# High and low halves of x as one moving operand in 44 projections

## The chip, the cores and the metric

One core of a Trainium2 chip. The metric is the device time of one execution in microseconds (us). The engines go by their names in the profile: PE (TensorE, matrix multiplications), PEld (its weight loads), DVE (VectorE), ACT (ScalarE), POOL (GpSimd) and SP (SyncE, which issues the DMAs of the weights). SBUF is the on-chip memory; PSUM holds the results of PE, here in 8 banks of 128 x 512 floats.

## The reference, cut to what matters

Two stacks run one after the other on `x` of 256 positions by 1024 features, two layers each. The first has five branches in each layer (stick-breaking attention, mLSTM, gated MLP, retention, attention to a memory), the second a mixer or a conformer convolution, cross attention to a second memory, and a convolutional feed-forward. In single precision:

```
proj = rms_norm(x, norm_pre) @ w_in            # (256, 1024) @ (1024, d_in), split into 21 parts
y_gm = spatial_gating(gelu(gm_u), gelu(gm_v), ...)   # times silu(gm_z)
q, k = rotary(rt_q), rotary(rt_k)              # retention
...
h = rms_norm_2(x, norm) @ w_up                 # (256, 1024) @ (1024, 6144)
g = causal_dwconv(h[..., :3072], dw_w, dw_b)   # three taps in time
x = x + (gelu(g) * h[..., 3072:]) @ w_down
```

Nearly all the work is products of a 256 x 1024 (or 512) activation with a weight matrix that is read from HBM once.

## The kernel before

Activations lie with features on partitions and the S = 256 positions along the free axis, in chunks of 128 features. To keep single precision on PE, each operand is split into a high and a low part of a reduced format (fp32r): `Operand` (L244) holds `h` and `l`, written by ACT (a rounding copy) and DVE (the rest, by subtraction, L254 and L259). `weights` (L285) brings a weight block by one DMA on SP into a tile of the pool `wraw` (5 tiles) and splits it into `wh` (ACT, L297) and `wl` (DVE, L298), 128x1024 each, of the pool `whl` (4 tiles). The splits carry a higher priority in the scheduler (`ahead`), so that they stand some way ahead of their use.

A product is three matmuls for each chunk k of the inner axis and each block m of 128 output features, all into one PSUM region: `wh` by `xh`, `wh` by `xl`, `wl` by `xh`. In `mm_F` (L302) the weight is the stationary operand (128x128) and x the moving one, 256 columns wide. `proj_F` (L328) runs it for 512 output features: two banks (`psF`), each with two blocks m of 256 columns, two weight tiles for each half of the inner axis, each [128, 2, 512]. After it, DVE multiplies each bank by the row of norms `rb` into SBUF (`scaled_F`, L344, L347). `mm_T` (L314) is the other form, x stationary and weights moving, 512 columns wide (`psT`). Down and output projections use `mm_F` with banks called `psO`.

The banks come from two pools of four, `mbank` (mm) and `bank` (aux), each in rotation: a bank's next user waits until its last reader is done. `mid` is a piece of other work that `proj_F` calls before the second half of its inner axis. Work elsewhere that the change touches: the sigmoid gates with `silu2_F` (L365), the rotations of retention (`rot`, three DVE products out of each bank, L714 to L716), the keys of the memory attention (`kv_k`, L922) and the feed-forward (`conv_ffn`, L1198): for each of 6 slices a `gx` and a `u` projection, then taps, a gelu and the product, and a down projection of the slice before.

Each engine runs its instructions in order. The order on every engine is set when the program is built, by a list scheduler that places instructions by its own estimate of times and the priorities; nothing is reordered on the chip. So an instruction that waits holds up all that stand behind it on its engine.

Of the kernel before, what the change touches and what calls it, by code (L numbers as in the profile page):

```python
# [11 lines left out]
F32 = mybir.dt.float32  # L12
F32R = mybir.dt.float32r
# [5 lines left out]
S = 256  # L19
# [35 lines left out]
def stack_kernel(ctx: ExitStack, tc: tile.TileContext, I: dict, out: bass.AP):  # L55
# [188 lines left out]
    class Operand:  # L244


        def __init__(self, n, pool, tag):
            self.h = pool.tile([128, n, S], F32R, tag=tag + "h", name=tag + "h")
            self.l = pool.tile([128, n, S], F32R, tag=tag + "l", name=tag + "l")

        def put(self, c, src):
            hi, lo = self.h[:, c], self.l[:, c]
# [49 lines left out]
    def mm_F(pss, src, op, k0, n_k, first, last):  # L302

        w = made.pop() if made else weights(src, n_k)
        for m in range(src.shape[1] // 128):
            for k in range(n_k):
                wh, wl = w[k][0][:, m * 128:m * 128 + 128], w[k][1][:, m * 128:m * 128 + 128]
                xh, xl = op.h[:, k0 + k], op.l[:, k0 + k]
                for n, (a, b) in enumerate(((wh, xh), (wh, xl), (wl, xh))):
                    PE.matmul(pss[m // 2][:, m % 2], a, b,  # L310
                              start=(first and m % 2 == 0 and k == 0 and n == 0),
                              stop=(last and k == n_k - 1 and n == 2), skip_group_check=True)

    def mm_T(pss, src, op, k0, n_k, first, last, extra=None):  # L314

        w = weights(src, n_k)
        for t in range(2):
            sl = slice(t * 128, t * 128 + 128)
            for k in range(n_k):
                xh, xl = op.h[:, k0 + k, sl], op.l[:, k0 + k, sl]  # L320
                wh, wl = w[k]
                for n, (a, b) in enumerate(((xh, wh), (xl, wh), (xh, wl))):
                    PE.matmul(pss[t], a, b, start=(first and k == 0 and n == 0),  # L323
                              stop=(last and k == n_k - 1 and n == 2), skip_group_check=True)
                    if extra is not None and n < 2:
                        extra(t, k0 + k, n, a)
# [22 lines left out]
    def F_plain(w, c0, op, rb, name, dst=None, pss=None):  # L349
        if pss is None:  # L350
            pss = proj_F(w, c0, op)
        if dst is None:
            dst = t_f4([128, 4, S], name)
        scaled_F(pss, rb, dst)
        return dst

    def T_plain(w, c0, op, rc, name, dst=None, extra=None):
        pss = proj_T(w, c0, op, extra=extra)
        if dst is None:
            dst = t_f4([128, 2, 512], name)  # L360
        for t in range(2):
            A.activation(dst[:, t], pss[t], AF.Copy, scale=rc[:, t:t + 1])
        return dst

    def silu2_F(w, c0, op, rb, name, pss=None):  # L365

        z = F_plain(w, c0, op, rb, name, pss=pss)
        th = t_f4([128, 4, S], name + "_t")
        A.activation(th, z, AF.Tanh, scale=0.5)
        V.scalar_tensor_tensor(z, th, 1.0, z, op0=ALU.add, op1=ALU.mult)  # L370
        return z
# [111 lines left out]
    def layer(l, nrm, early, kv, late, nxt):  # L483
# [32 lines left out]
        def sb_branch():  # L516
# [35 lines left out]
                                        compare_op=ALU.is_ge, fill=0.0, base=-1,  # L552
                                        channel_multiplier=-1)

            pss_z = proj_F(w, OFF["sb_z"], op, mid=later)
            z = silu2_F(w, OFF["sb_z"], op, rb, "sbz", pss=pss_z)
            o = Operand(4, yop, "y")
            for i in range(2):
                ps = bank([128, 2, S], "ps_sbo")
# [142 lines left out]
        def rt_branch():  # L702
# [3 lines left out]
            V.tensor_tensor(sr, sinF, rb, op=ALU.mult)  # L706

            def rot(c0, name):
                pss = proj_F(w, c0, op)
                q = t_f4([128, 4, S], name)  # L710
                x = t_f4([128, 4, S], name + "_x")
                for i in range(2):
                    sl = slice(2 * i, 2 * i + 2)
                    V.tensor_tensor(q[:, sl], pss[i], bc(cr, 2), op=ALU.mult)  # L714
                    V.tensor_tensor(x[0:64, sl], pss[i][64:128], bc(sr[64:128], 2), op=ALU.mult)
                    V.tensor_tensor(x[64:128, sl], pss[i][0:64], bc(sr[0:64], 2), op=ALU.mult)  # L716
                V.tensor_tensor(q, q, x, op=ALU.add)
                return q

# [46 lines left out]
        def gm_branch(ws):  # L766
# [17 lines left out]
            for t in range(2):  # L784
# [1 line left out]
                                op1=ALU.mult)  # L786
                V.tensor_tensor(v[:, t], v[:, t], lng[:, 0], op=ALU.mult)
                V.tensor_tensor(v[:, t], v[:, t], lng[:, 1], op=ALU.add)
            u = F_plain(w, OFF["gm_u"], op, rb, "gmu")
# [21 lines left out]

        def xa_branch():
            kF, vT = kv()
            qF = F_plain(w, OFF["xa_q"], op, rb, "xaq")
# [106 lines left out]

    def kv_k(op, rb, w, c0):  # L922
        was, ahead[0] = ahead[0], KV_AHEAD
        k = F_plain(w, c0, op, rb, "kF", kvp.tile([128, 4, S], F32, tag="kv", name="kF"))
        ahead[0] = was
        return k

# [270 lines left out]
    def conv_ffn(l, nrm, nxt):  # L1198
# [9 lines left out]

        for n in range(6):
            get = bank if n else mbank  # L1210
            pg = proj_F(wu, 512 * n, op, get=get)
            if n == 0:
                rc, row = nrm.column(), []
            pu = proj_F(wu, 3 * D + 512 * n, op, get=get,
                        mid=None if n else lambda: row.append(row_of(rc, "x")))
            rb = row[0]
            gx = t_f4([128, 4, S], "f_gx")
            scaled_F(pg, rb, gx)
# [5 lines left out]
            u = t_f4([128, 4, S], "f_u")  # L1224
            o = Operand(4, yop, "y")
            for i in range(2):
                sl = slice(2 * i, 2 * i + 2)
                V.tensor_tensor(u[:, sl], pu[i], bc(rb, 2), op=ALU.mult)
# [182 lines left out]
```

## Time and profile before

| | |
|---|---|
| median of 3 runs | 1823.22 us (1822.25 to 1824.26) |
| profiled execution, own time | 1826.32 us |
| its span, first to last instruction | 1824.6 us |
| PE busy | 1788.9 us, 98% of the span |
| PE weight loads | 1666.0 us, 91% |
| DVE busy | 1265.6 us, 69% |
| ACT busy | 958.9 us, 53% |
| POOL busy | 60.8 us, 3% |
| read from HBM | 306.53 MB, 169 GB/s over the span |

An engine's busy time counts the union of its records. Records of matmuls overlap, since a matmul is shown from its start to the modelled end of a pipeline, so the pace of PE is read from starts. An idle engine that is not waited for costs nothing.

### The profile page before, as it was taken

How to read it: one execution, taken by the hardware profiler on the slowest of the kernel's cores; microseconds unless marked ns; L12 is line 12 of the kernel's file. 1: busy time of each engine (PE TensorE's matmuls, PEld its weight loads, DVE VectorE, ACT ScalarE, POOL GpSimd, SP SyncE). 2: the span in 40 equal slices, each digit the busy share in tenths (PEclk: the TensorE clock that was granted, in tenths of full speed). 3: DMA queues.
4: the chain of work that ended last, by engine and by line, in shares of the span. 5: the costliest groups of instructions: out<-in, count | busy, mean ns of one | idle time of the engine just before them, and what ended most of it. 6: DMA issues, size and time to landing. Idle time of an engine off the chain costs nothing. (4 is left out here: it accounts for less than half of the span.)

```text
span 1824.6 us, 30483 instructions
## 1 busy us (share of the span) xinstructions
PE 1788.9 (98%) x12255; PEld 1666.0 (91%) x12255; DVE 1265.6 (69%) x1888; ACT 958.9 (53%) x1369; POOL 60.8 (3%) x91
## 2 busy tenths in 40 slices
PE   8899999999999999999999999999999989999998
PEld 8889998888999898888899998999999989899998
DVE  6587856676667877656657965676669985577666
ACT  5755335554556443455455854455457545455443
POOL 0000001100000100000000000000000000000000
PEclk9999999999999999999999999999999999999999
DMA  7456554666554655467655554455554344355552
GB/s 222 131 167 208 168 174 147 202 206 193 165 173 146 185 176 169 149 197 232 207 169 178 156 169 144 155 181 178 183 183 146 103 133 151 116 180 184 183 184 93
DMA packets 162654, 309.57 MB, mean 170 GB/s; under 512 B 10852, under 2 KB 19504, under 8 KB 162512
## 3 DMA queue, kind: packets, MB, share of 16 engines
q1 hardware_dynamic: 159872, 302.04, 52.7%
q0 software_dynamic: 2128, 5.37, 1.0%
q8 instruction: 96, 1.57, 0.4%
q14 instruction: 46, 0.38, 0.1%
q10 hardware_dynamic: 512, 0.21, 0.1%
HBM read 306.53 MB, written 1.05 MB: 169 GB/s over the span
## 5 line engine op out<-in xcount | busy, mean ns | idle before, releaser
L298 DVE TENSOR_TENSOR wl<-raw,wh 128x1024 fp32r<-128x1024 f32 x558 | 668.6, 1222 | 343.8 <-ACT wh L297 335.4
L297 ACT ACTIVATE wh<-raw 128x1024 fp32r<-128x1024 f32 x558 | 573.2, 1054 | 529.9 <-PE psF L310 178.4
L310 PE MATMUL psF<-xh,wh 128*128 128x256 f32 x1888 | 538.4, 285 | 3.5 <-ACT wh L1302 3.3
L310 PE MATMUL psF<-xh,wl 128*128 128x256 f32 x1888 | 536.1, 284 | 0.8 <-DVE wl L298 0.8
L310 PE MATMUL psF<-xl,wh 128*128 128x256 f32 x1888 | 536.7, 284 | 0.0
L310 PEld LDWEIGHTS psF<-xh,wh 128*128 128x128 f32 x1888 | 363.7, 193 | 4.5 <-ACT wh L1302 3.6
L310 PEld LDWEIGHTS psF<-xl,wh 128*128 128x128 f32 x1888 | 364.0, 193 | 1.5 <-issue 1.0
L310 PEld LDWEIGHTS psF<-xh,wl 128*128 128x128 f32 x1888 | 363.3, 193 | 1.6 <-DVE wl L298 1.4
L310 PE MATMUL psO<-yh,wh 128*128 128x256 f32 x800 | 227.6, 285 | 6.0 <-ACT yh L253 6.0
L310 PE MATMUL psO<-yl,wh 128*128 128x256 f32 x800 | 227.3, 284 | 0.0
L310 PE MATMUL psO<-yh,wl 128*128 128x256 f32 x800 | 227.0, 284 | 0.3 <-DVE wl L298 0.3
L323 PE MATMUL psT<-wl,xh 128*128 128x512 f32 x544 | 216.3, 398 | 0.0
L323 PE MATMUL psT<-wh,xl 128*128 128x512 f32 x544 | 216.0, 397 | 0.0
L323 PE MATMUL psT<-wh,xh 128*128 128x512 f32 x544 | 214.5, 394 | 0.0
L310 PEld LDWEIGHTS psO<-yh,wh 128*128 128x128 f32 x800 | 154.2, 193 | 6.9 <-ACT yh L253 6.7
L310 PEld LDWEIGHTS psO<-yh,wl 128*128 128x128 f32 x800 | 154.3, 193 | 0.5 <-DVE wl L298 0.5
L310 PEld LDWEIGHTS psO<-yl,wh 128*128 128x128 f32 x800 | 154.3, 193 | 0.3
L323 PEld LDWEIGHTS psT<-wl,xh 128*128 128x128 f32 x544 | 102.7, 189 | 21.4
L323 PEld LDWEIGHTS psT<-wh,xl 128*128 128x128 f32 x544 | 102.8, 189 | 20.8
L323 PEld LDWEIGHTS psT<-wh,xh 128*128 128x128 f32 x544 | 102.8, 189 | 19.6
L1114 DVE SCALAR_TENSOR_TENSOR c_h<-c_a,cols,c_h 128x229 f32<-128x229 f32 (+15 forms) x144 | 63.2, 465 | 3.0
L323 PE MATMUL psT<-wl,yh 128*128 128x512 f32 x160 | 62.3, 389 | 0.0
(414 smaller groups left out, 2134.0 us busy)
## 6 DMA issues: line engine op xcount, KB each, us to landing
raw<-in_w_in SPq DMA_DIRECT2D x224, 512.0 KB, 4.3
raw<-in_f_w_up SPq DMA_DIRECT2D x96, 512.0 KB, 4.3
raw<-in_f_w_down SPq DMA_DIRECT2D x48, 512.0 KB, 4.3
raw<-in_w_up SPq DMA_DIRECT2D x40, 512.0 KB, 4.0
raw<-in_c_w_pw SPq DMA_DIRECT2D x24, 512.0 KB, 3.9
raw<-in_ab_w_in SPq DMA_DIRECT2D x20, 512.0 KB, 4.4
raw<-in_w_mem_kv SPq DMA_DIRECT2D x16, 512.0 KB, 3.9
raw<-in_w_out SPq DMA_DIRECT2D x16, 512.0 KB, 3.6
```

What stands on the lines that cost most here:

```text
L297: A.activation(hi, raw, AF.Copy)
L298: V.tensor_tensor(lo, raw, hi.bitcast(F32), op=ALU.subtract)
L310: PE.matmul(pss[m // 2][:, m % 2], a, b, start=(first and m % 2 == 0 and k == 0 and n == 0), stop=(last and k == n_k - 1 and n == 2), skip ...
L323: PE.matmul(pss[t], a, b, start=(first and k == 0 and n == 0), stop=(last and k == n_k - 1 and n == 2), skip_group_check=True)
L1114: V.scalar_tensor_tensor(h[:, j:], a[:, m, 0:S - j], col("c_dw_w_2", (30 - j) * 8 + c), h[:, j:], op0=ALU.mult, op1=ALU.add)
```

## The change

`Operand` puts `h` and `l` side by side in one tile `hl` ([128, n, 2, 256]), so that both halves of a chunk can be read as one row of 512. A new `proj_P` uses it: for each (k, m), `wh` is multiplied with `hl` (512 columns, into a whole bank: the product with the high part in half 0, with the low part in half 1), and `wl` with `h` (256 columns, into half 0). Each block m has a bank of its own, so a projection takes four banks, in two groups g of 256 output features with two banks each. The weights of a group come in tiles of [128, 4, 256]: the same number and size of DMAs, with contiguous stretches of 1 KB rather than 2 KB. At the end of a group ACT copies half 0 of each bank to SBUF and DVE adds half 1 to it; the multiplication by `rb` (or the rotation) then works on SBUF. `mid` runs after the first group. It is used for `gx` and `u` of the feed-forward (24 projections), the keys `kv_k` (6) and, in each of the first stack's layers, `sb_z`, `gm_u`, `gm_z`, `rt_q`, `rt_k`, `xa_q`, `xa_z` (14 together). The other projections stay as they are.

```diff
 class Operand:
-            self.h = pool.tile([128, n, S], F32R, tag=tag + "h", name=tag + "h")
-            self.l = pool.tile([128, n, S], F32R, tag=tag + "l", name=tag + "l")
+            self.hl = pool.tile([128, n, 2, S], F32R, tag=tag + "hl", name=tag + "hl")
+            self.h, self.l = self.hl[:, :, 0], self.hl[:, :, 1]
...
+    def proj_P(w, c0, op, dst, mid=None, get=None):
+        for g in range(2):
+            pss = [(get or mbank)([128, 2, S], "psP") for _ in range(2)]
+            for k0 in (0, 4):
+                ws = weights(w[k0 * 128:(k0 + 4) * 128, c0 + g * 256:c0 + g * 256 + 256], 4)
+                for m in range(2):
+                    for k in range(4):
+                        wh, wl = (t[:, m * 128:m * 128 + 128] for t in ws[k])
+                        PE.matmul(pss[m], wh, op.hl[:, k0 + k], start=(k0 + k == 0), stop=False,
+                                  skip_group_check=True)
+                        PE.matmul(pss[m][:, 0], wl, op.h[:, k0 + k], start=False,
+                                  stop=(k0 + k == 7), skip_group_check=True)
+            for m in range(2):
+                A.activation(dst[:, 2 * g + m], pss[m][:, 0], AF.Copy)
+                V.tensor_tensor(dst[:, 2 * g + m], dst[:, 2 * g + m], pss[m][:, 1], op=ALU.add)
+            if mid and g == 0:
+                mid()
+        return dst
...
+    def P_plain(w, c0, op, rb, name, dst=None, mid=None):
...
+        proj_P(w, c0, op, dst, mid)
+        for i in range(2):
+            sl = slice(2 * i, 2 * i + 2)
+            V.tensor_tensor(dst[:, sl], dst[:, sl], bc(rb, 2), op=ALU.mult)
...
-            pss_z = proj_F(w, OFF["sb_z"], op, mid=later)
-            z = silu2_F(w, OFF["sb_z"], op, rb, "sbz", pss=pss_z)
+            z = silu2_F(w, OFF["sb_z"], op, rb, "sbz", mid=later)
...
-                pss = proj_F(w, c0, op)
-                q = t_f4([128, 4, S], name)
+                q = proj_P(w, c0, op, t_f4([128, 4, S], name))
...
-                    V.tensor_tensor(q[:, sl], pss[i], bc(cr, 2), op=ALU.mult)
-                    V.tensor_tensor(x[0:64, sl], pss[i][64:128], bc(sr[64:128], 2), op=ALU.mult)
-                    V.tensor_tensor(x[64:128, sl], pss[i][0:64], bc(sr[0:64], 2), op=ALU.mult)
+                    V.tensor_tensor(x[0:64, sl], q[64:128, sl], bc(sr[64:128], 2), op=ALU.mult)
+                    V.tensor_tensor(x[64:128, sl], q[0:64, sl], bc(sr[0:64], 2), op=ALU.mult)
+                    V.tensor_tensor(q[:, sl], q[:, sl], bc(cr, 2), op=ALU.mult)
...
-            pg = proj_F(wu, 512 * n, op, get=get)
+            gx = proj_P(wu, 512 * n, op, t_f4([128, 4, S], "f_gx"), get=get)
...
-            pu = proj_F(wu, 3 * D + 512 * n, op, get=get,
-                        mid=None if n else lambda: row.append(row_of(rc, "x")))
+            u = proj_P(wu, 3 * D + 512 * n, op, t_f4([128, 4, S], "f_u"), get=get,
+                       mid=None if n else lambda: row.append(row_of(rc, "x")))
```

In the whole program PE has 1408 matmuls fewer (1408 of 512 columns and 1408 of 256 in place of 4224 of 256), ACT 176 copies more and DVE 176 additions more. Since the scheduler sets the order, the order of other instructions moves too; three places follow. Rows are in the order of the engine: the line, the operation, output and inputs (a number after a name tells one tile from another), and the size. `wl_` is the low part of a weight tile, `raw_` its loaded form.

PE, first layer, from the last step of `gm_z` over the mixing matmuls of the gated MLP (`ps_mix`) to the first step of `rt_q` (two blocks m in a bank `psF` before, one in a bank `psP` now). Before:

```order
L310 MATMUL psF_1806<-xh_114,wh_1875 128x256
L310 MATMUL psF_1806<-xl_115,wh_1875 128x256
L310 MATMUL psF_1806<-xh_114,wl_1876 128x256
L799 MATMUL ps_mix_1936<-gm_w_1579,gmv_1661 128x128 x4
L799 MATMUL ps_mix_1946<-gm_w_1579,gmv_1661 128x128 x4
L310 MATMUL psF_1960<-xh_114,wh_1964 128x256
L310 MATMUL psF_1960<-xl_115,wh_1964 128x256
L310 MATMUL psF_1960<-xh_114,wl_1965 128x256
```

Now:

```order
L324 MATMUL psP_1809<-xhl_114,wh_1834 128x512
L326 MATMUL psP_1809<-xhl_114,wl_1835 128x256
L827 MATMUL ps_mix_1865<-gm_w_1553,gmv_1635 128x128 x4
L827 MATMUL ps_mix_1875<-gm_w_1553,gmv_1635 128x128 x4
L324 MATMUL psP_1890<-xhl_114,wh_1894 128x512
L326 MATMUL psP_1890<-xhl_114,wl_1895 128x256
```

A step is two matmuls in place of three, and the mixing matmuls stand where they stood.

DVE, first layer, from the end of `gm_z` to the first use of the bank of `rt_q` (`gmu` and `gmz` are the gated MLP's parts, `gm_mx` its mixed values, `yl` or `yhl` the operand written from it, `rt_c` and `rt_s` the rotation tables). Before:

```order
L370 SCALAR_TENSOR_TENSOR gmz_1927<-gmz_t_1930,gmz_1927 128x1024
L805 TENSOR_TENSOR gm_mx_1941<-ps_mix_1936,gm_bs_1585 128x512
L792 TENSOR_TENSOR gmu_1801<-gmu_1801,gmz_1927 128x1024
L805 TENSOR_TENSOR gm_mx_1951<-ps_mix_1946,gm_bs_1585 128x512
L807 TENSOR_TENSOR gmu_1801<-gmu_1801,gm_mx_1941 128x512
L807 TENSOR_TENSOR gmu_1801<-gmu_1801,gm_mx_1951 128x512
L705 TENSOR_TENSOR rt_c_1956<-cosF_111,x_rb_392 128x256
L706 TENSOR_TENSOR rt_s_1957<-sinF_112,x_rb_392 128x256
L259 SCALAR_TENSOR_TENSOR yl_1935<-gmu_1801,yh_1934 128x512 x2
L298 TENSOR_TENSOR wl_2096<-raw_2093,wh_2095 128x1024
L298 TENSOR_TENSOR wl_2102<-raw_2099,wh_2101 128x1024
L714 TENSOR_TENSOR rtq_2082<-psF_1960,rt_c_1956 128x512
```

Now:

```order
L384 TENSOR_TENSOR gmz_1757<-gmz_1757,x_rb_391 128x512
L734 TENSOR_TENSOR rt_c_1885<-cosF_111,x_rb_391 128x256
L735 TENSOR_TENSOR rt_s_1886<-sinF_112,x_rb_391 128x256
L400 SCALAR_TENSOR_TENSOR gmz_1757<-gmz_t_1860,gmz_1757 128x1024
L298 TENSOR_TENSOR wl_2004<-raw_2001,wh_2003 128x1024
L820 TENSOR_TENSOR gmu_1653<-gmu_1653,gmz_1757 128x1024
L298 TENSOR_TENSOR wl_2026<-raw_2023,wh_2025 128x1024
L835 TENSOR_TENSOR gmu_1653<-gmu_1653,gm_mx_1870 128x512
L835 TENSOR_TENSOR gmu_1653<-gmu_1653,gm_mx_1880 128x512
L298 TENSOR_TENSOR wl_2054<-raw_2051,wh_2053 128x1024
L259 SCALAR_TENSOR_TENSOR yhl_1864<-gmu_1653,yhl_1864 128x2x256 x2
L330 TENSOR_TENSOR rtq_1889<-rtq_1889,psP_1890 128x256
```

The first read of the bank of `rt_q` (`psP_1890`) stands at the end of both; ahead of it there are now three weight splits among the chain where there were two behind it, and a multiplication of `gmz` that came before this piece. In the rows just before these, `gm_mx_1870`, one more split, an addition of `gmz` and `gm_mx_1880` also follow the end of the projection.

DVE in the conformer, towards the last `c_acc`, which PE's means wait for (`c_h` are taps of the convolution, `kF` the keys of the second memory). Before:

```order
L298 TENSOR_TENSOR wl_14837<-raw_14834,wh_14836 128x1024
L1114 SCALAR_TENSOR_TENSOR c_h_13865<-c_a_14540,cols_110,c_h_13865 128x230
L347 TENSOR_TENSOR kF_14640<-psF_14642,mem_rb_8129 128x512
L1114 SCALAR_TENSOR_TENSOR c_h_13865<-c_a_14540,cols_110,c_h_13865 128x229
L1114 SCALAR_TENSOR_TENSOR c_h_13865<-c_a_14540,cols_110,c_h_13865 128x228
L1114 SCALAR_TENSOR_TENSOR c_h_13865<-c_a_14540,cols_110,c_h_13865 128x227
L1114 SCALAR_TENSOR_TENSOR c_h_13865<-c_a_14540,cols_110,c_h_13865 128x226
L1121 TENSOR_TENSOR c_acc_14890<-c_acc_14890,c_h_13865 128x512
L298 TENSOR_TENSOR wl_14957<-raw_14954,wh_14956 128x1024
L298 TENSOR_TENSOR wl_14963<-raw_14960,wh_14962 128x1024
L347 TENSOR_TENSOR kF_14765<-psF_14766,mem_rb_8129 128x512
L347 TENSOR_TENSOR kF_14765<-psF_14767,mem_rb_8129 128x512
```

Now:

```order
L330 TENSOR_TENSOR kF_14048<-kF_14048,psP_14049 128x256
L1142 SCALAR_TENSOR_TENSOR c_h_13170<-c_a_13845,cols_110,c_h_13170 128x230
L1142 SCALAR_TENSOR_TENSOR c_h_13170<-c_a_13845,cols_110,c_h_13170 128x229
L298 TENSOR_TENSOR wl_14222<-raw_14219,wh_14221 128x1024
L1142 SCALAR_TENSOR_TENSOR c_h_13170<-c_a_13845,cols_110,c_h_13170 128x228
L330 TENSOR_TENSOR kF_14048<-kF_14048,psP_14050 128x256
L1142 SCALAR_TENSOR_TENSOR c_h_13170<-c_a_13845,cols_110,c_h_13170 128x227
L384 TENSOR_TENSOR kF_14048<-kF_14048,mem_rb_7761 128x512
L298 TENSOR_TENSOR wl_14252<-raw_14249,wh_14251 128x1024
L1142 SCALAR_TENSOR_TENSOR c_h_13170<-c_a_13845,cols_110,c_h_13170 128x226
L330 TENSOR_TENSOR kF_14048<-kF_14048,psP_14099 128x256
L1149 TENSOR_TENSOR c_acc_14151<-c_acc_14151,c_h_13170 128x512
```

The keys' eviction is now spread in additions and multiplications, and the additions of the second keys' banks (`kF_14048`) with two splits stand ahead of the last `c_acc`, where before they followed it.

## Rows read from the trace of the kernel before

**Rows 1.** The page's head and its first part: busy time and share by engine.

```profile
span 1824.6 us, 30483 instructions
...
PE 1788.9 (98%) x12255; PEld 1666.0 (91%) x12255; DVE 1265.6 (69%) x1888; ACT 958.9 (53%) x1369; POOL 60.8 (3%) x91
```

**Rows 2.** PE's waits: what for, us in total, times, longest us.

```profile
PE psO L310 <- ACT yh L253: 6.0, 2, 4.9
...
PE ps_sbo L567 <- POOL sb_zs L551: 1.3, 2, 0.9
...
PE psF L310 <- DVE wl L298: 0.8, 2, 0.5
```

**Rows 3.** Timeline of PE in the last feed-forward: start us, us, instruction (256 columns).

```profile
1700.81 0.28 PE L310 MATMUL psF<-xh,wh 128*128 128x256 f32 x1
...
1703.93 0.28 PE L310 MATMUL psF<-xh,wl 128*128 128x256 f32 x1
```

**Rows 4.** Timeline of PE in the second layer: the 512-wide form.

```profile
842.62 0.39 PE L323 MATMUL psT<-wh,xl 128*128 128x512 f32 x1
...
845.79 0.39 PE L323 MATMUL psT<-wh,xh 128*128 128x512 f32 x1
```

**Rows 5.** Stretches: length; PE, PEld, DVE, ACT, POOL busy; clock, DMA share, GB/s.

```profile
186.40:211.20 24.80, 24.80 (x210) 24.80 (x209) 23.75 (x29) 10.01 (x12) 0.00 (x0) 1.00 0.53 168
...
1200.00:1300.00 100.00, 100.00 (x836) 100.00 (x835) 65.54 (x80) 46.92 (x63) 0.00 (x0) 1.00 0.57 182
1460.40:1488.10 27.70, 27.70 (x194) 26.90 (x195) 25.08 (x47) 6.14 (x7) 0.00 (x0) 1.00 0.32 99
```

**Rows 6.** Timeline of PE at two seams between the forms.

```profile
163.15 0.39 PE L323 MATMUL psT<-wl,xh 128*128 128x512 f32 x1
163.38 0.28 PE L310 MATMUL psF<-xh,wh 128*128 128x256 f32 x1
...
211.11 0.28 PE L310 MATMUL psF<-xh,wl 128*128 128x256 f32 x1
211.23 0.40 PE L323 MATMUL psT<-wh,xh 128*128 128x512 f32 x1
```

**Rows 7.** Groups of DVE: busy us, mean ns of one, then idle before.

```profile
L235 DVE TENSOR_TENSOR sqacc<-sqacc,sq 128x256 f32<-128x256 f32 x12 | 5.1, 421 | 0.2
```

**Rows 8.** Groups of ACT, a copy out of PSUM.

```profile
L197 ACT ACTIVATE x_rb<-ps_rb 128x256 f32<-128x256 f32 x8 | 3.0, 369 | 2.6 <-PE ps_rb L194 2.6
```

**Rows 9.** Timeline of DVE from the gated MLP to retention, first layer.

```profile
186.61 0.69 DVE L347 TENSOR_TENSOR gmz<-psF,x_rb 128x512 f32<-128x512 f32 x1 [2.19 <-PE psF L310]
...
198.46 0.68 DVE L714 TENSOR_TENSOR rtq<-psF,rt_c 128x512 f32<-128x512 f32 x1
```

**Rows 10.** Timeline of DVE in the conformer: the last `c_acc`.

```profile
1482.66 0.69 DVE L1121 TENSOR_TENSOR c_acc<-c_acc,c_h 128x512 f32<-128x512 f32 x1
```

**Rows 11.** The page's DMA issues: KB each, us to landing.

```profile
raw<-in_c_w_pw SPq DMA_DIRECT2D x24, 512.0 KB, 3.9
```

**Rows 12.** Timeline of PE from the gated MLP to retention, first layer.

```profile
186.41 1.95 PE L799 MATMUL ps_mix<-gm_w,gmv 128*128 128x128 f32 x16
188.12 0.36 PE L310 MATMUL psF<-xh,wh 128*128 128x256 f32 x1
```

**Rows 13.** The chain that ended last, in the conformer: start us, us, what.

```profile
1460.40 10.56 PE ps_conv L1103 x50
...
1488.11 0.86 PE ps_mean L1124 x4
```

**Rows 14.** Timeline of DVE at the entry of the first feed-forward.

```profile
1163.08 0.69 DVE L942 TENSOR_TENSOR xF<-xF,psO 128x512 f32<-128x512 f32 x1 [0.81 <-PE psO L310]
...
1168.09 0.47 DVE L259 SCALAR_TENSOR_TENSOR xl<-xF,cols,xh 128x256 fp32r<-128x256 f32 x1
```

**Rows 15.** The page's costliest groups: busy us, mean ns of one, then idle before.

```profile
L298 DVE TENSOR_TENSOR wl<-raw,wh 128x1024 fp32r<-128x1024 f32 x558 | 668.6, 1222 | 343.8 <-ACT wh L297 335.4
L297 ACT ACTIVATE wh<-raw 128x1024 fp32r<-128x1024 f32 x558 | 573.2, 1054 | 529.9 <-PE psF L310 178.4
```

More of the change, by code (lines that the diff above doesn't have):

```diff
@@ L355, in F_plain @@
         return dst
+    def P_plain(w, c0, op, rb, name, dst=None, mid=None):
+        if dst is None:
+            dst = t_f4([128, 4, S], name)
+        proj_P(w, c0, op, dst, mid)
+        for i in range(2):
+            sl = slice(2 * i, 2 * i + 2)
+            V.tensor_tensor(dst[:, sl], dst[:, sl], bc(rb, 2), op=ALU.mult)
+        return dst
     def T_plain(w, c0, op, rc, name, dst=None, extra=None):
@@ L363, in T_plain, with silu2_F @@
         return dst
-    def silu2_F(w, c0, op, rb, name, pss=None):
-        z = F_plain(w, c0, op, rb, name, pss=pss)
+    def silu2_F(w, c0, op, rb, name, mid=None):
+        z = P_plain(w, c0, op, rb, name, mid=mid)
         th = t_f4([128, 4, S], name + "_t")
@@ L788, in gm_branch @@
                 V.tensor_tensor(v[:, t], v[:, t], lng[:, 1], op=ALU.add)
-            u = F_plain(w, OFF["gm_u"], op, rb, "gmu")
+            u = P_plain(w, OFF["gm_u"], op, rb, "gmu")
             A.activation(u, u, AF.Gelu_apprx_tanh)
@@ L813, in xa_branch @@
             kF, vT = kv()
-            qF = F_plain(w, OFF["xa_q"], op, rb, "xaq")
+            qF = P_plain(w, OFF["xa_q"], op, rb, "xaq")
             ps = [softmax([(qF[:, h], kF[:, h])], 128.0 ** -0.5) for h in range(NH)]
@@ L923, in kv_k @@
         was, ahead[0] = ahead[0], KV_AHEAD
-        k = F_plain(w, c0, op, rb, "kF", kvp.tile([128, 4, S], F32, tag="kv", name="kF"))
+        k = P_plain(w, c0, op, rb, "kF", kvp.tile([128, 4, S], F32, tag="kv", name="kF"))
         ahead[0] = was
@@ L1210, in conv_ffn @@
             get = bank if n else mbank
-            pg = proj_F(wu, 512 * n, op, get=get)
+            gx = proj_P(wu, 512 * n, op, t_f4([128, 4, S], "f_gx"), get=get)
             if n == 0:
                 rc, row = nrm.column(), []
-            pu = proj_F(wu, 3 * D + 512 * n, op, get=get,
-                        mid=None if n else lambda: row.append(row_of(rc, "x")))
+            u = proj_P(wu, 3 * D + 512 * n, op, t_f4([128, 4, S], "f_u"), get=get,
+                       mid=None if n else lambda: row.append(row_of(rc, "x")))
             rb = row[0]
-            gx = t_f4([128, 4, S], "f_gx")
-            scaled_F(pg, rb, gx)
+            for i in range(2):
+                sl = slice(2 * i, 2 * i + 2)
+                V.tensor_tensor(gx[:, sl], gx[:, sl], bc(rb, 2), op=ALU.mult)
             g = t_f4([128, 4, S], "f_g")
@@ L1223, in conv_ffn @@
                 A.activation(g[:, m], g[:, m], AF.Gelu_apprx_tanh, bias=col("f_dw_b_2", l * 24 + c))
-            u = t_f4([128, 4, S], "f_u")
             o = Operand(4, yop, "y")
@@ L1227, in conv_ffn @@
                 sl = slice(2 * i, 2 * i + 2)
-                V.tensor_tensor(u[:, sl], pu[i], bc(rb, 2), op=ALU.mult)
+                V.tensor_tensor(u[:, sl], u[:, sl], bc(rb, 2), op=ALU.mult)
                 V.tensor_tensor(u[:, sl], u[:, sl], g[:, sl], op=ALU.mult)
```

## Prediction

> **What bounds the kernel now.** I read the page's first two lines first: PE is busy for 98% of the span, every other engine is well below [rows 1]. So PE's own pace is the bound, and an edit counts by what it takes from PE or by the gaps it opens there. The table of PE's waits comes next: its longest entry is 6.0 us in 1.8 ms, and the one for a weight split (`wl`) comes to 0.8 us in all [rows 2]. Weights are ready ahead of PE almost everywhere.
>
> The busy figure of one matmul misleads: records overlap. The timeline shows starts. Between the 256-wide matmuls at 1700.81 and 1703.93 lie 26 steps in 3.12 us, 0.120 us each, while each is shown as 0.28 long [rows 3]. Between the 512-wide ones at 842.62 and 845.79 lie 14 steps in 3.17 us, 0.2264 us each [rows 4]. At 2.4 GHz, the level of a granted clock of 1.00 [rows 5], 256 columns are 106.7 ns and 512 are 213.3 ns. Both widths thus cost about 13 ns beyond their columns. That 13 ns is what this change saves, once for every two matmuls that it merges.
>
> **What is removed.** A (k, m) step is three 256-wide matmuls, 3 x 0.120 = 0.360 us. It becomes one 512-wide and one 256-wide, 0.2264 + 0.120 = 0.346 us. The new stream alternates widths, which the old one never does for long, so I looked for seams: a 256-wide starts 0.23 us after a 512-wide (163.15 to 163.38), a 512-wide 0.12 us after a 256-wide (211.11 to 211.23) [rows 6]. Nothing extra is paid at a change of width, so I take 13 ns a step (13.6 from the two counts, rounded down). The order of the new program holds 1408 such steps: 24 feed-forward projections, 14 of the layers and 6 of keys, 44 x 32. Gain: 1408 x 0.013 = **18.3 us**. Bounds for a step: 0.360 if the 512-wide pass costs two 256-wide ones (gain 0), and 0.320, the bare columns of 768 at 2.4 GHz (gain 56); the seams put it next to 0.346.
>
> The Trainium skill ("TensorE: Matmul & The Clock Gate", section "Back-to-back issue gap") speaks against this gain: an isolated matmul is spaced N/2.4 + 2.5 ns. By that a step would save 2.5 ns, 3.5 us in all (an estimate from the page). The 120 and 226 ns of [rows 3, 4] disagree by some 11 ns a matmul, so the trace decides. The same section gives 131 ns sustained for N = 512; the rows do not bear that out either.
>
> **What is added off PE.** Each projection gets 4 ACT copies and 4 DVE additions of 128x256, 176 of each. The nearest rows are 421 ns for a DVE addition of that size and 369 ns for an ACT copy of it out of PSUM [rows 7, 8]: 74 us of DVE and 65 us of ACT. DVE goes from 69% [rows 1] to about 74% of the span. The multiplication by `rb` moves from PSUM to SBUF operands: 0.69 us for the `gmz` one that reads PSUM, 0.69 for the `c_acc` one that reads SBUF, both 128x512 [rows 9, 10]: nothing. In the steady feed-forward DVE is 66% busy [rows 5]; a block of 34.6 us (two projections, 64 x 0.36, and a down projection, 96 x 0.12) gets 8 x 0.42 = 3.4 us each, which makes some 77%. A group there lasts 16 x 0.346 = 5.5 us and the copies and additions of its two banks take 2 x 0.37 + 2 x 0.42 = 1.6 us, so cover is ample: I cost it at nothing there. If the cover were gone, it would cost what rival B says.
>
> DMAs: the same number and bytes; rows of 1 KB rather than 2 KB. Such transfers exist (`c_w_pw`), at 3.9 us to landing [rows 11], and the DMA engines are 57% busy in the feed-forward [rows 5]. Nothing. SP issues the same count and is moved past nothing else. `mid` now runs between the column groups, at half of the projection as before; nothing.
>
> **Where PE will wait.** Four places have DVE full or a chain exposed; each costs part of the gain.
>
> 1. *Gating to retention, both layers.* From 186.4 to 211.2 DVE is busy 23.75 of 24.80 us and PE never waits [rows 5]. Before, DVE goes from the second `gmz` multiplication at 186.61 to the first `rtq` eviction at 198.46, 11.85 us [rows 9], and PE needs that bank back only for the key projection. In the new order (shown above) the first `rtq` addition stands behind the gate's second half (copy, addition, 512-wide multiplication), the tables, four weight splits, the tanh chain and the `yhl` subtractions. Summed from the end of `gmz`'s last matmul: `gm_mx` can only follow `ps_mix` (1.0), 0.6 for it, 1.1 for a split, 0.4 addition, 0.6, 0.6 multiplication, tanh chain to 6.7, then split, gate, split, two gates, split (5.8) and the two subtractions (1.2), so the bank is read at 14 and free at 14.4. PE asks for it after `ps_mix` (188.12 - 186.41 = 1.7 [rows 12]) and two groups of 5.55: 12.8. Wait 1.6 us, and some 0.4 at `ps_blk`, where two more DVE steps stand before the last rotation: 2 us a layer, the second layer taken alike. **Loss 4**, bounds 0 (the order's slack suffices) and 8.
>
> 2. *Conformer.* PE runs `ps_conv` at 1460.40, then projections, and reaches `ps_mean` at 1488.11, 27.7 us later [rows 13]; it needs the `c_acc` of 1482.66, done at 1483.35 [rows 10], 22.95 us after the start. DVE is busy for 25.08 of these 27.70 us [rows 5]. In the new order 7 additions (7 x 0.42 = 2.9), one more multiplication (0.7), two more splits (2.3) and one more `c_acc` addition (0.7) stand ahead of that last `c_acc`: 6.6 us. It is then done at 29.6, and `ps_mean` starts 1.9 us later than before; and what PE gains ahead of it, up to 0.9 us of the 18.3 (two key projections, 64 x 0.013), is not seen either. **Loss 2.8**, bounds 0 and 5.
>
> 3. *Stick-breaking, both layers.* PE already waits for POOL's mask, 1.3 us in two [rows 2], with the `sb_z` projection as its filler. A filler half lasts 5.55 rather than 5.76, so the wait grows by what the filler lost, and a copy and an addition come before the gate's tanh: about 0.75 us a layer. **Loss 1.5**, bounds 0 and 3.
>
> 4. *Feed-forward entries, both layers.* The last operand chunk's low part comes at 1168.09 + 0.47, 5.5 us after the release at 1163.08 [rows 14]. The new order has PE at that chunk after some 6.5 us, with one weight split now ahead of the last parts: 0 to 1 us each. **Loss 1**, bounds 0 and 2.
>
> Sum: -18.3 + 4 + 2.8 + 1.5 + 1 = **-9.0 us**. The profiled execution took 1826.3 us (span 1824.6), 3.1 above the median 1823.2 of the runs; it would come to 1817.3, and the median to **1814.2**.
>
> **Rivals.** *A, everything hides.* The four waits vanish in slack that I undercounted. For it: PE's waits are small today [rows 2]. Against it: DVE is 96 and 91% busy in places 1 and 2 [rows 5]. 1823.2 - 18.3 = 1805.
>
> *B, DVE and ACT become the bound.* A group's banks are free only after ACT's copy and DVE's addition. If both stand behind a pair of weight splits (2 x 1.05 on ACT, 2 x 1.22 on DVE [rows 15]) the eviction takes 2.1 + 0.74 + 2.4 + 0.84 = 6.1 us, over the 5.55 that the other two banks cover. It decides from there: 0.55 us a group, in half of the 88 groups 24 us of wait, 1814 + 24 = 1838. For it: the evictions are now two steps on two engines that also carry every weight. Against it: 66% of DVE in the feed-forward [rows 5], where 24 of the 44 lie.
>
> *C, the gap is 2.5 ns.* Then the spacing of [rows 3, 4] is set by something that the wide pass does not remove, as by the weight load for each 256 columns. Gain 3.5 us less 9.3: 1829. Against it: the seams [rows 6]. That is the result that the Trainium skill's isolated formula (same page and section) would give.
>
> *D, the wide pass is no cheaper than two.* Reading two halves as one operand costs 2 x 0.120; only the losses stay: 1823.2 + 9.3 = 1832.5. Against it: the 512-wide rows [rows 4], though their moving operand is a weight tile.
>
> *E, the losses double.* The hand counts of places 1 to 4 come out near their upper bounds (18 in all): 1823.
>
> **How the numbers follow.** Forecast, losses between 5 and 13: 0.58 (its own range 1810 to 1818). A: 0.20. E: 0.12. B: 0.05. C: 0.02. D: 0.03. A measurement of this kernel can tell 0.2% (3.6 us) from no change: faster means under 1819.6, slower over 1826.9. The forecast and A are faster, and a fifth of E: 0.80. The rest of E is the same: 0.10. B, C and D are slower: 0.10. The range that leaves out B to D and the far half of E is 1804 to 1820.5.
>
> **What would show it.** Right: in the profile after, a 512-wide start to a 256-wide start of 0.227 and back of 0.120; the spans of feed-forward projections shorter by 0.42 us each; PE's waits for evictions in the list at the retention and conformer places, about 2 us each, and few elsewhere. Wrong: a step of 0.36 (D) or 0.357 (C); a table of PE waits with `psP` behind DVE additions in the feed-forward (B); no such entry at all (A). The forecast fails first if the wait at retention is not there, since it is almost half of the losses.

## The result and the profile after

The changed kernel is slower by 0.9%. Its median is 1839.72 us (6 runs, 1837.99 to 1842.04) against 1822.74 us for the kernel before (6 runs, 1821.84 to 1828.76): a ratio of 1.0088, 95% interval 1.0073 to 1.0103. The forecast was 1814.2, range 1804.0 to 1820.5. The profiled execution has a span of 1838.8 us and a mean granted clock of 0.988, where before had 1824.6 and 0.993.

The head of the page and its first part, to be set beside [rows 1]: busy us, share, instructions.

```profile
span 1838.8 us, 28040 instructions
...
PE 1786.5 (97%) x10847; PEld 1595.0 (87%) x10847; DVE 1328.3 (72%) x2064; ACT 1020.5 (55%) x1545; POOL 62.2 (3%) x91
```

PE has 1408 matmuls less and yet nearly the busy time of before, in a span that is 14 us longer: its busy time fell little, and it stands still more. PE's waits in the changed kernel (us in total, times, longest us) say where, against [rows 2]:

```profile
PE psT L344 <- DVE kF L330: 6.1, 1, 6.1
PE psO L310 <- ACT yhl L253: 6.0, 2, 4.9
PE psP L324 <- DVE kF L330: 6.0, 1, 6.0
PE ps_rows L633 <- DVE gi L627: 3.2, 1, 3.2
...
PE psP L324 <- DVE rtq L330: 2.4, 2, 1.2
...
PE ps_rb L194 <- POOL cln_rc L112: 1.4, 1, 1.4
```

The second entry is that of before. Three are new: two of 6 us for an addition of `kF`, the keys of a memory, and the retention wait that the prediction had placed, 1.2 us in each layer. The wait for `gi` is in layer 1; the kernel before has a wait at `ps_rows` in layer 0 instead, 3.3 us, which is 1.1 here. Three smaller ones grew: for the last norm of the conformer (`cln_rc`) from 0.5 to 1.4 us, for the sums at the layer ends (`post_rc`) from 0.9 to 2.6, for weight splits from 0.8 to 2.3.

To see where time was lost I compared the start of the same matmul in both traces, which gives this table (worked out from the two timelines of PE). What a stretch loses is its slip:

| stretch, by PE's landmarks in the kernel before | start before, after | lost in it, us |
|---|---|---|
| start to the sums at the end of layer 0 (`ps_rb` of `post_rc`) | 490.8, 485.9 | -4.9 |
| end of layer 0, to the entry of layer 1 (`ps_ss`) | 521.3, 524.4 | +8.0 |
| to the first rows of the mLSTM, layer 1 (`ps_rows`) | 569.1, 570.9 | -1.2 |
| mLSTM's rows and columns, to its blocks (`ps_blk`) | 606.3, 616.5 | +8.4 |
| to the sums at the end of layer 1 | 951.2, 962.5 | +1.1 |
| end of layer 1 (`ps_ss`) | 982.3, 1001.7 | +8.1 |
| mixer, cross attention and first feed-forward (`ps_mem`) | 1371.1, 1387.3 | -3.3 |
| conformer (`ps_rb` of `cln_rc`) | 1500.0, 1516.9 | +0.8 |
| to the output (`ps_out`), second feed-forward in it | 1814.6, 1828.7 | -2.7 |

Three places of 8 us make the loss. The first row is no measure of the change: e3 and e4 (below), which keep the old form there, gained 6.7 and 2.3 us in it. A part that varies is the granted clock. Before, it read 0.72 over 86 to 92 us and 0.62 over 107 to 116, 1.7 + 3.4 = 5.1 us lost; in the changed kernel 1.00 over 86 to 92 and 0.66 over 104 to 109, 1.7 us lost.

The first of the three places is the end of layer 0. The timeline of DVE and PE there in the changed kernel (start, length, engine, what, and the idle time before it with its releaser):

```profile
492.19 0.68 DVE L913 TENSOR_TENSOR oF<-oF,post_rb 128x512 f32<-128x512 f32 x1
...
498.59 0.69 DVE L915 TENSOR_TENSOR xF<-xF,oF 128x512 f32<-128x512 f32 x1
499.20 0.75 DVE L330 TENSOR_TENSOR kF<-kF,psP 128x256 f32<-128x256 f32 x2
...
499.75 1.19 PE L344 MATMUL psT<-wh,mhl 128*128 128x512 f32 x2 [6.09 <-DVE kF L330]
```

PE has finished both groups of the keys by 493.7 and wants a bank for the values (`psT`). The keys hold all four banks of the pool mm. The addition that frees the first stands behind nearly all of the layer's closing norm on DVE (`oF`, `xF`, most of the new operand), at 499.20. At the end of layer 1 it is the same, but there the next taker is another key projection (the second memory's), which wants banks for its own `psP`. In the kernel before, DVE reached the keys no sooner:

```profile
503.54 0.68 DVE L347 TENSOR_TENSOR kF<-psF,mem_rb 128x512 f32<-128x512 f32 x1
...
509.60 0.68 DVE L347 TENSOR_TENSOR kF<-psF,mem_rb 128x512 f32<-128x512 f32 x1
```

PE had gone on to the values meanwhile, in the timeline of before:

```profile
498.91 0.40 PE L323 MATMUL psT<-wh,mh 128*128 128x512 f32 x1
```

The two evictions came 4.6 and 10.7 us after that. But the keys held two banks, the values took the other two, and nobody waited.

The granted clock falls during this wait and stays low behind it. Stretches: the length, then PE's busy time, with the clock third from the end; the first three rows are of the changed kernel, the last two of the one before:

```profile
498.00:500.00 2.00, 0.24 (x1) 0.28 (x2) 2.00 (x6) 0.69 (x2) 0.00 (x0) 0.50 0.65 231
...
500.00:506.00 6.00, 6.00 (x18) 4.73 (x19) 3.37 (x8) 0.74 (x2) 0.00 (x0) 0.64 0.00 0
...
578.00:590.00 12.00, 12.00 (x54) 10.42 (x53) 5.90 (x8) 6.22 (x13) 1.83 (x3) 0.57 0.21 68
```

```profile
500.00:506.00 6.00, 6.00 (x29) 4.94 (x28) 6.00 (x11) 3.83 (x9) 0.00 (x0) 1.00 0.57 180
578.00:590.00 12.00, 12.00 (x102) 12.00 (x102) 8.51 (x15) 7.74 (x16) 1.83 (x3) 1.00 0.69 219
```

At 0.64 over 6 us, 6 x 0.36 = 2.2 us more are lost (an estimate): 6.1 + 2.2 = 8.3, near the slip of 8.0 at the end of layer 0. The mLSTM's 8.4 has the same two parts: 3.2 us of wait, and 12 x 0.43 = 5.2 us of lost clock, which here fell only some 4 us after the wait had ended. The wait comes from here (PE, then DVE in order):

```profile
574.41 0.27 PE L633 MATMUL ps_rows<-ident,gi 128*4 128x128 f32 x1 [3.22 <-DVE gi L627]
```

```profile
570.88 0.41 DVE L330 TENSOR_TENSOR sbz<-sbz,psP 128x256 f32<-128x256 f32 x1
...
572.73 1.23 DVE L298 TENSOR_TENSOR wl<-raw,wh 128x1024 fp32r<-128x1024 f32 x1
573.87 0.41 DVE L330 TENSOR_TENSOR sbz<-sbz,psP 128x256 f32<-128x256 f32 x1
574.20 0.16 DVE L627 SCALAR_TENSOR_TENSOR gi<-gi,fa 128x8 f32<-128x8 f32 x1
```

PE wants `gi`; its short chain of 128x8 steps is interleaved with the new additions of `sbz` and a split. e7 below shows that `sb_z` brings this wait; which of these instructions makes it was not tested.

### The profile page after: what moved, and what is told of

It is laid out like the page before. It is cut to its first block, busy times and chain, and to the rows that moved or that the text cites. A ratio compares the mean times of both kernels' runs of the same rounds, so it can differ in the third digit from the quotient of the medians.

```text
span 1838.8 us, 28040 instructions
## 1 busy us (share of the span) xinstructions
PE 1786.5 (97%) x10847; PEld 1595.0 (87%) x10847; DVE 1328.3 (72%) x2064; ACT 1020.5 (55%) x1545; POOL 62.2 (3%) x91
## 5 line engine op out<-in xcount | busy, mean ns | idle before, releaser
L324 PE MATMUL psP<-xhl,wh 128*128 128x512 f32 x1216 | 430.2, 398 | 2.5 <-DVE rtq L330 2.4
L344 PE MATMUL psT<-wh,xhl 128*128 128x512 f32 x1088 | 344.0, 396 | 0.0
L326 PE MATMUL psP<-xhl,wl 128*128 128x256 f32 x1216 | 340.5, 281 | 0.0
L310 PE MATMUL psO<-yhl,wh 128*128 128x256 f32 x1600 | 292.4, 285 | 6.0 <-ACT yhl L253 6.0
L324 PEld LDWEIGHTS psP<-xhl,wh 128*128 128x128 f32 x1216 | 228.4, 188 | 58.0 <-ACT wh L297 3.0
L310 PEld LDWEIGHTS psO<-yhl,wh 128*128 128x128 f32 x1600 | 250.4, 191 | 7.6 <-ACT yhl L253 6.7
L310 PE MATMUL psF<-xhl,wh 128*128 128x256 f32 x1344 | 251.7, 289 | 2.8 <-ACT wh L1330 2.6
L326 PEld LDWEIGHTS psP<-xhl,wl 128*128 128x128 f32 x1216 | 229.6, 189 | 0.6
L310 PE MATMUL psO<-yhl,wl 128*128 128x256 f32 x800 | 227.2, 284 | 0.3 <-DVE wl L298 0.3
L344 PE MATMUL psT<-wl,xhl 128*128 128x512 f32 x544 | 215.8, 397 | 0.0
```

The source lines that it names most:

```text
L310: PE.matmul(pss[m // 2][:, m % 2], a, b, start=(first and m % 2 == 0 and k == 0 and n == 0), stop=(last and k == n_k - 1 and n == 2), skip ...
L324: PE.matmul(pss[m], wh, op.hl[:, k0 + k], start=(k0 + k == 0), stop=False, skip_group_check=True)
L326: PE.matmul(pss[m][:, 0], wl, op.h[:, k0 + k], start=False, stop=(k0 + k == 7), skip_group_check=True)
```

## Experiments

In what follows the wide form is `proj_P`, the old form `proj_F`. The theory after this reading: the loss at the layer ends is a matter of banks. `proj_P` takes four banks where `proj_F` took two, so at the layer ends the next projection waits for an eviction that was late before, too. The rivals: that DVE and ACT carry too much there (load), and that it is the second step of the eviction (the addition behind ACT's copy), not the count of banks.

The runs were made in several sets, in which the kernel before came to between 1821.96 and 1822.97 us; ratios go by the kernel before of the same set, while a difference in us between two experiments is good to about 1 us.

**e1, the keys in the old form.**

```diff
-        k = P_plain(w, c0, op, rb, "kF", kvp.tile([128, 4, S], F32, tag="kv", name="kF"))
+        k = F_plain(w, c0, op, rb, "kF", kvp.tile([128, 4, S], F32, tag="kv", name="kF"))
```

> The changed kernel with the six key projections kv_k back in the old form (three matmuls, two banks, one multiplication out of PSUM). In the trace of the changed kernel PE waits 6.1 and 6.0 us at the two layer ends for a kF addition, and the times there slip by 8.0 and 8.1 us with the granted clock that falls behind them. Theory (the four banks): both waits go, 16 us less, 6 x 32 steps of 10 ns are given up again, 1.9 us: 1839.7 - 16 + 2 = 1826. The rival (load: DVE and ACT simply have too much to do at the layer ends) gives the same here, less exactly; the rival that the waits only move to the next reader of a late addition gives 1836 to 1840 with new entries in PE's waits.

Measured: 1821.13 us, beside 1822.97 for before (ratio 0.9995, 0.9986 to 1.0005). The six key projections, 1/7 of the change, cost 18.6 us; the rest of it gains 1.8 us by the medians and by its interval perhaps nothing. It came out 5 us below the expectation. In its trace the mLSTM of layer 1 slips by 5.0 us, not 8.4; that trace is of the fastest of its ten executions (1816.81), so the rest of the difference is open.

**e5, the keys alone.** The kernel before with `kv_k` alone in the wide form.

> The kernel before with the wide form in the six key projections alone. Theory (the four banks): the two waits of 6 us at the layer ends come back by this part alone, with the slips of 8 us; 6 x 32 x 0.010 = 1.9 us are gained: 1823 + 16 - 2 = 1837. If the waits need the load of the other wide projections beside them, the time is 1821 to 1826.

Measured: 1842.47 us, ratio 1.0106 (1.0093 to 1.0119). The keys do it without any load from the other projections, and PE's waits are those of the full change:

```profile
PE psT L344 <- DVE kF L330: 6.1, 1, 6.1
...
PE psP L324 <- DVE kF L330: 5.7, 1, 5.7
```

It is 3 us above the changed kernel, which has the gains of the other 38 projections to set against it, and 5 above the expectation; the slips at its layer ends are 8.5 and 9.3 us.

**e2, two of the keys' banks from the other pool.**

```diff
+    def split_banks():
+        left = [mbank, mbank, bank, bank]
+        return lambda shape, name: left.pop(0)(shape, name)
...
-        k = P_plain(w, c0, op, rb, "kF", kvp.tile([128, 4, S], F32, tag="kv", name="kF"))
+        k = kvp.tile([128, 4, S], F32, tag="kv", name="kF")
+        proj_P(w, c0, op, k, get=split_banks())
```

> The changed kernel with one edit: of a key projection's four banks two come from the pool mm and two from the pool aux, so that vT, the projection behind it, finds two free banks in mm as it did before. All copies and additions stay. Theory (the four banks): PE's waits for kF at both layer ends go, about 16 us less: 1824. Rival (load on DVE and ACT at the layer ends): the waits stay or come back as a wait of a later instruction: 1836 to 1840.

Measured: 1823.20 us, 16.5 less than the changed kernel, with every copy and addition in place. In its trace (PE, then DVE) the values start at 493.28 with no wait, and the first addition of the keys comes at 500.11, later than in the changed kernel:

```profile
493.28 0.63 PE L348 MATMUL psT<-wh,mhl 128*128 128x512 f32 x2
```

```profile
500.11 0.42 DVE L334 TENSOR_TENSOR kF<-kF,psP 128x256 f32<-128x256 f32 x1
```

So at the layer ends it is not the load on DVE that costs, but the bank.

**e6, four banks and no additions.** On the base of e3 (below), the old three matmuls for the keys, one bank for each block m, evicted by one multiplication:

```diff
+        pss = [mbank([128, 2, S], "psK") for _ in range(4)]
...
+                    for n, (p, q) in enumerate(((wh, xh), (wh, xl), (wl, xh))):
+                        PE.matmul(pss[m][:, 0], p, q, start=(k0 + k + n == 0),
+                                  stop=(k0 + k == 7 and n == 2), skip_group_check=True)
+        for m in range(4):
+            V.tensor_tensor(dst[:, m], pss[m][:, 0], rb, op=ALU.mult)
```

> As e3 (feed-forward alone in the wide form), with the key projections in the old three matmuls and no copies or additions, but one bank for each block of 128 features, four in all, each evicted by one multiplication of 128x256 out of PSUM. Theory (it is the number of banks): PE waits at both layer ends for a kF multiplication before the next projection, 4 to 6 us each, and 10 to 16 us are lost against e3: 1826 to 1832. Rival (it is the second step of the eviction, the addition behind ACT's copy): the waits stay away, 1816 to 1818.

Measured: 1831.24 us, 15.3 more than e3. Its slips at the two layer ends are 8.2 and 7.7 us. The count of banks alone brings the loss back. The wait in its trace, with DVE's first eviction:

```profile
499.15 1.19 PE L344 MATMUL psT<-wh,mhl 128*128 128x512 f32 x2 [5.03 <-ACT xhl L258]
```

```profile
498.59 0.42 DVE L963 TENSOR_TENSOR kF<-psK,mem_rb 128x256 f32<-128x256 f32 x1
```

The profile names `xhl` of ACT as the releaser, but PE starts 0.14 us after the multiplication of `kF` ends (498.59 + 0.42 = 499.01), and the matmul reads nothing of `xhl`: this is a name to be read with care; by e2, e6 and e9 together the bank is the cause.

**e9, the same four banks, freed early.** The changed kernel with the copies and additions of the keys at the scheduler's priority of their weights:

```diff
+            with tc.high_priority(offset=ahead[0] if ahead[0] == KV_AHEAD else 0):
                 for m in range(2):
                     A.activation(dst[:, 2 * g + m], pss[m][:, 0], AF.Copy)
```

> The changed kernel with its four banks for each key projection as they are, but with the copies and additions of the key projections given the scheduler's priority of the key weights, so that on DVE they stand ahead of most of the norm's work at the layer ends and not behind it. Theory (four banks, and a bank that is freed late because its addition stands behind the norm): PE's waits for kF fall from 6 us to under 2, the norm's chain is pushed back by the four additions, 1.5 us: 1824 to 1828. Rival (four banks alone, whatever DVE's order): 1838 to 1841.

Measured: 1821.52 us, ratio 0.9995 (0.9986 to 1.0004), 18.2 less than the changed kernel, a larger gain than expected. The additions now stand between the norm's steps, and the values do not wait (DVE, then PE):

```profile
487.17 0.41 DVE L331 TENSOR_TENSOR kF<-kF,psP 128x256 f32<-128x256 f32 x1
489.84 0.41 DVE L331 TENSOR_TENSOR kF<-kF,psP 128x256 f32<-128x256 f32 x1
```

```profile
493.12 0.64 PE L345 MATMUL psT<-wh,mhl 128*128 128x512 f32 x2
```

Both halves of the cause are thus shown: four banks (e2, e6) and an eviction that stands late in DVE's order (e9). Either one removed is enough.

**e3, the wide form in the feed-forward alone** (24 projections; keys, gates, `sb_z` and rotations in the old form).

> The wide form in the 24 feed-forward projections alone, everything else as before the change (operands in one tile). A step of the wide form is 0.350 us in the trace of the changed kernel (0.233 + 0.117) against 0.360, so 24 x 32 x 0.010 = 7.7 us less than before: 1815, and no new wait of PE. Rival (the additions on DVE and copies on ACT delay the weights or the evictions in the feed-forward): 1819 to 1823.

Measured: 1815.97 us, ratio 0.9966 (0.9953 to 0.9979). No new wait of PE for an eviction. The feed-forward carries its 96 copies and 96 additions for nothing. The medians give 7.0 us for 768 steps, 9 ns each; in the trace the two feed-forwards, from the first to the last start of their 12 wide projections, last 181.8 and 182.3 us where before each lasted 185.1. That is 6.0 us, 8 ns a step.

**e4, the matmuls regrouped**, on the base of e3: four wide ones, then four narrow ones.

```diff
                     for k in range(4):
-                        wh, wl = (t[:, m * 128:m * 128 + 128] for t in ws[k])
+                        wh = ws[k][0][:, m * 128:m * 128 + 128]
                         PE.matmul(pss[m], wh, op.hl[:, k0 + k], start=(k0 + k == 0), stop=False,
                                   skip_group_check=True)
+                    for k in range(4):
+                        wl = ws[k][1][:, m * 128:m * 128 + 128]
                         PE.matmul(pss[m][:, 0], wl, op.h[:, k0 + k], start=False,
                                   stop=(k0 + k == 7), skip_group_check=True)
```

> As e3, with the matmuls of a block regrouped: the four wide ones with wh first, then the four narrow ones with wl, so that the width changes twice in eight matmuls and not each time. If the 3.5 ns by which a step misses 0.2264 + 0.120 comes from alternating, the spacing goes to 0.227 and 0.120 and 24 x 32 x 0.0035 = 2.7 us go: 1812. If it belongs to the wide matmul with this operand whatever stands beside it, the spacing stays 0.233 and 0.117 or the like, and the time is that of e3.

Measured: 1815.53 us (ratio 0.9963, 0.9950 to 0.9976), that of e3 within its interval. Its timeline of PE, four matmuls in a row:

```profile
1700.27 1.09 PE L324 MATMUL psP<-xhl,wh 128*128 128x512 f32 x4
1701.20 0.63 PE L328 MATMUL psP<-xhl,wl 128*128 128x256 f32 x4
1701.67 1.09 PE L324 MATMUL psP<-xhl,wh 128*128 128x512 f32 x4
```

Four wide ones take 0.93 us, 0.2325 each, four narrow ones 0.47, 0.1175 each: 0.350, as when they alternate. The two feed-forwards in its trace last 181.6 us each, 0.9 us less than in e3 in all, where 2.7 had been expected if the alternation were the cause: it is not most of what a step misses.

**e10, rotations** (e3 and `rt_q`, `rt_k` wide) and **e7, `sb_z`** (e3 and `sb_z` wide).

> As e3, with the wide form also in rt_q and rt_k of both layers, which the prediction gave 2 us of waits a layer. By the prediction 4 us of loss less 4 x 32 x 0.010 = 1.3 of gain: 1816.0 + 2.7 = 1818.7. Rival (the wait of 1.2 us for the rtq addition is all that is lost): 1816.0 + 2.4 - 1.3 = 1817.1.

Measured: 1819.13 us (runs from 1816.2 to 1822.3), 3.2 more than e3: nearer to the first number than to the rival's. Its trace speaks for less. The waits for `rtq` are shorter there than in the changed kernel:

```profile
PE psP L324 <- DVE rtq L330: 1.1, 2, 0.5
```

From the mLSTM's blocks to the sums at the layer end its trace is 0.7 and 0.8 us longer than before, in net, and that of e3 0.0 and 0.1: so the rotations cost about 1.4 us there, near the rival's 2.4 - 1.3 = 1.1, and the rest of the 3.2 lies elsewhere.

> As e3, with the wide form also in the two sb_z projections. In the trace of the changed kernel, and of e1 and e2, the time from the later mask of layer 1 to its mLSTM blocks slips by 5 to 9 us, with a granted clock of 0.5 for 6 to 16 us. Theory (the rearranged order around sb_z opens the gap after which the clock falls): 5 to 8 us lost against e3: 1821 to 1824. Rival (something else in the layers, or chance from one execution to the next): the time of e3, 1815.5 to 1816.5.

Measured: 1819.14 us, also 3.2 more than e3, where 5 to 8 had been expected. Its runs spread from 1816.8 to 1823.9, more than those of e3 (1815.2 to 1817.8). In its trace PE's wait for `gi` is 3.2 us as in the changed kernel, but the clock is low for less time behind it (0.57 over 566 to 570 us, then 1.00). It falls at this place without that wait too: in e3, with `sb_z` in the old form, it reads 0.66 over 571 to 576 us, and the stretch slips by 1.5 us, against 5.0 in e7. How long it is low differs from execution to execution, and that is probably the spread. This was not tested apart.

**e8, e11, e12, other choices of projections.** e8 is the changed kernel with the keys' banks split as in e2, `sb_z` and rotations old; e11 the wide form in the feed-forward and the gates `gm_u`, `gm_z`, `xa_q`, `xa_z`; e12 is e11 with the keys as in e9.

> The changed kernel with the key projections on two pools of banks as in e2, and sb_z, rt_q and rt_k back in the old form; gm_u, gm_z, xa_q and xa_z of both layers stay wide, as do the keys and the feed-forward. If these 14 projections only give their 10 ns a step, 14 x 32 x 0.010 = 4.5 us less than e3: 1811.5. If each eviction in two steps costs its chain more than the projection gains, 1816 to 1820.

> The wide form in the feed-forward and in gm_u, gm_z, xa_q and xa_z of both layers; keys, sb_z and the rotations in the old form. If the places that lose are left out and the others give 10 ns a step: e3 less 8 x 32 x 0.010 = 2.6, 1813.4. If the gates' longer chains take it back: 1816 to 1817.

> e11 (feed-forward and the gates gm_u, gm_z, xa_q, xa_z in the wide form) with the key projections wide too, their copies and additions at the priority of their weights as in e9. If the keys' waits are gone for good: e11 less 6 x 32 x 0.010 = 1.9, 1811.8. If the longer chain of the norm at the layer ends and of the conformer (0.9 us in each of three places in the traces of e2 and e9) takes it back: 1813.5 to 1816.

Measured: e8 1817.33 us (ratio 0.9966, 0.9954 to 0.9978), e11 **1813.67 us** (0.9954, 0.9942 to 0.9967), e12 1816.46 us (0.9963, 0.9950 to 0.9977). e11 met its expectation and is the fastest here; e8 came out in its second range, e12 0.5 us above its own. Without the wait wide keys still save nothing: against the same kernel with old keys e9 and e2 are 0.4 and 2.1 us slower (e1), e12 and e8 2.8 and 3.7 (e11). In the traces of e2 and e8 the sums at the end of layer 1 and the conformer's last norm each come 0.9 us later after their `ps_ss` than before, and the conformer's mean 0.4 and 0.5 us later after `ps_conv`, in e12 2.1.

## Why the prediction was wrong

Set side by side, with the runs' medians: feed-forward -7.0 (e3), gates -2.3 (e11 less e3), rotations +3.2 (e10 less e3), `sb_z` +3.2 (e7 less e3), keys +18.6 (the changed kernel less e1). The sum is +15.7, measured +17.0.

Part of these differences is clock. Averaged over a kernel's runs, (1 - mean granted clock) x span is about 10 us for the kernel before (9.4 to 10.1 by set) and 22 for the changed one; it is 8.7 in e3, 9.1 in e11, 10.7 in e10, 12.3 in e7, 11.6 in e8, 12.0 in e12 and 16.0 in e6. This is an estimate of what the clock took, too high where PE waited anyway. By it some 1.4 of e3's 7.0 us are a better clock, 2.0 of the rotations' 3.2, all of the 3.2 of `sb_z`, half of e6's 15.3, and most of what e8 and e12 lost against e11. The prediction, which multiplied steps and added waits, has no term for the clock.

**The step that failed** is the list of places where PE will wait: it has four, and the keys at the layer ends, which cost 18.6 us, are not among them. "What is added off PE" counted DVE's and ACT's time and found cover, in a steady stretch of the feed-forward; it never asked what the two more banks of a projection take from its neighbours. The cover was real there (DVE 81% busy, forecast 77, and PE busy throughout):

```profile
1200.00:1300.00 100.00, 100.00 (x644) 90.72 (x643) 81.40 (x123) 62.76 (x103) 0.00 (x0) 1.00 0.61 186
```

The row that told it was there to read in the trace of before: the `kF` multiplications at 503.54 and 509.60, 4.6 and 10.7 us after PE had begun the next projection, with nobody waiting. An eviction that is late and harmless is a hidden debt, and doubling the banks calls it in. I looked at the order at the retention and conformer places because DVE was full there, and not at every place in which the pool turns over.

**The gain a step** was mis-sized: 13 ns forecast, 10 measured. The new stream, in the timeline of the changed kernel:

```profile
1700.87 0.40 PE L324 MATMUL psP<-xhl,wh 128*128 128x512 f32 x1
1701.10 0.28 PE L326 MATMUL psP<-xhl,wl 128*128 128x256 f32 x1
...
1702.28 0.40 PE L324 MATMUL psP<-xhl,wh 128*128 128x512 f32 x1
```

Four steps in 1.41 us are 0.352 each, where [rows 3, 4] gave 0.346; over the program the medians are 0.233 after a wide one and 0.117 after a narrow one, 0.350 a step. So 1408 steps give 14 us and not 18.3, and the feed-forwards of e3, by their length, 8 ns a step. The Trainium skill ("TensorE: Matmul & The Clock Gate", section "Back-to-back issue gap") would have given 3.5 us for all 1408 steps by its isolated formula (an estimate from the page); the two feed-forwards of e3 alone, 768 steps, are 6.0 us shorter, and 0.233 us is far from its 131 ns for N = 512.

**Retention** had the right place and mechanism, and somewhat too much loss: in the changed kernel 1.2 us of wait in each layer against 1.6 worked out, 0.25 against 0.4 at `ps_blk`. In e10 the waits for `rtq` were 0.5 us each and the stretches 1.4 us longer in all, 2.7 with the gain of their 128 steps, against a forecast loss of 4; that the median rose by 3.2, near the 2.7 expected, is in part luck.

**Stick-breaking** had the right place and the wrong victim: forecast 1.5, measured 3.2 plus the gain of its steps, 0.6. What is delayed is not the gate but the mLSTM's `gi`, which shares DVE with the new additions. In the changed kernel's trace 5.2 of the 8.4 us there are clock, and by the runs' granted clocks (above) so is all of the 3.2 by which the medians differ.

**The conformer** was over-sized: forecast 2.8. PE reaches `ps_mean` 27.9 us after `ps_conv` (1504.88 - 1476.99), against 27.7 in [rows 13]. The mechanism is there, as DVE's last `c_acc` shows:

```profile
1504.07 0.69 DVE L1149 TENSOR_TENSOR c_acc<-c_acc,c_h 128x512 f32<-128x512 f32 x1
```

It is done 27.8 us after `ps_conv` started, where that was 22.95 before and 29.6 had been forecast, and PE's means start right behind it. The hand count of DVE's steps was too long by 1.8 us. The **feed-forward entries** (forecast 1) show no new wait.

**Rival B** came close in its number, 1838, by accident: its place, late evictions in every second group, shows no wait. Its mechanism, a bank freed too late for the one who wants it, is the right one, in two places only. The chance of 0.10 for slower was too small because each rival was priced on stretches that I had already looked at.

## What to carry to other kernels

When an edit takes more buffers of a pool for the same work, go through every place where that pool turns over and ask who takes the next buffer and when the last reader of the one that it will now get runs; an eviction that was late for free becomes a wait. On PE, busy 98% of the time here, a wait cost twice, by itself and by the clock that fell with it (6.1 and 2.2 us); and since the clock differs between executions, a difference of 1 or 2 us between medians is to be read with the runs' granted clocks beside it. And a change made in 44 places is better tried in each kind of place: here 24 gave 7 us, 8 gave 2, and 6 lost 19 (in us, each good to about 1).

## What the runs showed of the hardware that was not expected

A 512-wide matmul with weights stationary and both halves of x moving starts the next one 0.233 us later, one with x stationary and a weight tile moving 0.227 [rows 4], in the same execution of the changed kernel too; a 256-wide one takes 0.117 to 0.118 beside it and 0.120 in the old stream [rows 3]. In e4, where the widths hardly alternate, it is 0.2325 and 0.1175; the cause stays open.

In a wait of 6.09 us of a PE that had been busy before, the granted clock went down to 0.50, the lower level (1.2 GHz), before the wait was over (498 to 500 us), and read 0.64 over the 6 us from 500 on. After 3.22 us of wait followed by a stretch of small matmuls it read 0.57 over 12 us; in e7, behind the same wait, 0.57 over 4 us and then 1.00.
